# Keys and a quarter of the queries by seven products, their results stored by GpSimd's queue, and the plain stage in an order written by hand

## The chip, the core and the metric

The kernel runs on one core of a Trainium2 chip. A time is the device time of one execution in microseconds (us). In the profile PE is TensorE (matmuls), PEld its weight loads, DVE VectorE, ACT ScalarE, POOL GpSimd and SP the engine that does nothing but issue DMAs; POOL and ACT issue DMAs too, each in a queue of its own.

## What is computed

One layer of a bidirectional encoder, on 512 + 256 tokens (two requests, shared weights), all in float32:

```python
h = rmsnorm(x, ln_mix_g); z = h @ w_in              # 2048 -> 2560 columns
zf, q, k, v = z[:, :1024], z[:, 1024:2048], z[:, 2048:2304], z[:, 2304:]
of = fourier_mix(zf, w_f)                           # 8 groups of 128 channels
oa = window_attention(rope(q), rope(k), v, sink)    # 16 heads, 4 of keys, +-128 tokens
x = x + concat(rmsnorm(of), rmsnorm(oa)) @ w_out
u = relu(rmsnorm(x, ln_mlp_g) @ w_up); x = x + (u * u) @ w_down
y = rmsnorm(x, ln_final_g)
```

## The kernel before

Every float32 operand of a matmul is split into a high part (ScalarE copies it to float32r) and a low part (VectorE subtracts the high part), and a product is three matmuls: high x high, high x low, low x high. A matmul has 128 x 128 weights and 384 token columns (`HALF`).

`w_in` is worked off in blocks of 256 columns, `w_in[0]` to `w_in[9]`. Blocks 0 to 3 are the Fourier channels, 4 to 7 the queries, 8 the keys, 9 the values. The stages, in order:

- *Values* (block 9), to 41 us.
- *Product stage* (41 to 157.5 us): a pair of blocks against both halves of x (2 x 2 blocks of columns c and of the inner dimension k, and 2 x 2 blocks of x) by seven products of sums instead of eight products (`names7`: a11, s1, s2, s3, a22, s4, a12). Two pairs g are worked, blocks (0, 1) and (2, 3). A *piece* n is half of one product's inner dimension for one pair, 24 matmuls; there are 28, in the order product, pair, half e. For each piece the weights are loaded on SP (`load7`, five pieces ahead), in four of the seven products summed on VectorE (`sum7`, three ahead), split (`high7` on ScalarE, three ahead, `low7` on VectorE, two ahead) and multiplied (`product7`). The x operands are summed and split on the way (`high_at`, `low_at`: tables of the piece at which each step stands). Results are taken out of PSUM after a piece with e = 1 (`out7`), by a copy on ScalarE or an add on VectorE, and stored to DRAM (`zf_d`) from ScalarE's queue one piece later. Within it the sums of squares of x's rows are made (`row_load` on GpSimd's queue, `row_square`, `row_norms`, `row_turn`, `row_spread`), whose outcome `rb` scales every column.
- *Plain stage* (157.5 to 361.3 us): blocks 8, 6, 4, 5, 7 by ordinary products, four pieces each, 20 pieces of 48 matmuls. Between them TensorE does the Fourier groups (`fold`, `stage1`, `stage2`), placed by `after(piece, ...)`; a fraction .5 is the middle of the next piece. Keys and queries are rotated (`cross` on GpSimd, `turned` on VectorE), split and stored (`parts`). TensorE's order is the program's; that of the other engines is a scheduler's, but for the last piece.
- *Attention and the first output projection* (from 361.3 us), by a table of times; `proj_slot` needs pieces of `w_out` from `out_load` and `out_split`, of which 0 to 2 are split in the plain stage and 3 (`out_split(3)`) just behind it.
- The second half of the projection and the MLP.

DMAs of one queue are issued in order, and an engine that waits holds up all that stands behind in its program.

Of the kernel before, what the change touches and what calls it, by code (L numbers as in the profile page):

```python
# [40 lines left out]
def hybrid_encoder(ctx: ExitStack, tc: tile.TileContext, a: dict):  # L41
# [75 lines left out]
    kr_d = dpool.tile([4 * P, T], F32, tag="k", name="k")  # L117
    qr_d = [[dpool.tile([2 * P, T], F32, tag=f"q{c}{i}", name=f"q{c}{i}") for c in "hl"] for i in range(NKV)]
# [79 lines left out]
    with ExitStack() as ph:  # L198
        hp = ph.enter_context(tc.tile_pool(name="hp", bufs=1, reuse_waits="tile"))
        pp = ph.enter_context(tc.tile_pool(name="pp1", bufs=4, space=PSUM))  # L200
# [7 lines left out]
        NP7 = 4 * len(names7)  # L208
# [5 lines left out]
        def load7(n):  # L214
            if n >= NP7:
                return
            x, g, e = names7[n // 4], n // 2 % 2, n % 2
            blocks = blocks7.get(x, (x,))
            raw7[n] = []
            for i, x in enumerate(blocks):  # L220
                if n < 2 or i > 0 or (len(blocks) == 1 and e == 1):
                    raw = wpool.tile([P, 4, 256], F32, tag="raw", name="raw", bufs=2)
                else:
                    raw = hq["p"].tile([P, 4, 256], F32, tag="wr", name="wr", bufs=3)
                c, k = int(x[1]) - 1, int(x[2]) - 1
                k0 = 8 * k + 4 * e
                nc.sync.dma_start(raw[:], w_in[2 * g + c][:, k0 : k0 + 4, :])
                raw7[n].append(raw)

        def sum7(n):  # L230
            if n >= NP7:
                return
            s, ge = names7[n // 4], n % 4
            x = raw7[n][0]
            if s == "s1":
                kept7[ge] = hq["p"].tile([P, 4, 256], F32, tag="ws", name="ws", bufs=4)
# [28 lines left out]
        def product7(n):  # L265
            w, g, e = n // 4, n // 2 % 2, n % 2
            bank = bank7[names7[w]]
            opens = w == 0 or names7[w] in ("s1", "a12")
            wh, wl = w7.pop(n)
            if e == 0 and opens:  # L270
                for r in range(2):
                    ps7[bank, g, r] = pp.tile([P, 512], F32, **(dict(tag="f", bufs=4) if bank == "Y" and 2 * g + r < 4 else dict(tag="ps", bufs=4)), name="p7")
            x = xs[w % 2]
            for i in range(4):
                for r in range(2):
                    for q, (l, o) in enumerate(((wh, 0), (wh, 1), (wl, 0))):
                        nc.tensor.matmul(  # L277
                            ps7[bank, g, r][:, :HALF], l[:, i, r * P : (r + 1) * P], x[:, o, 4 * e + i, :],
# [4 lines left out]
        def out7(n):  # L283
            while put7:
                put7.pop(0)()
            if n < 0 or n % 2 == 0:
                return
            s, g = names7[n // 4], n // 2 % 2
            c, t, how = take7[s]
            for r in range(2):  # L290
                ps = ps7[bank7[s], g, r][:, :HALF]
                if how == 1:
                    z = c7.pop((c, t, g, r))
                    nc.vector.tensor_tensor(out=z[:], in0=ps, in1=z[:], op=ALU.add)
                else:
                    z = hq["p"].tile([P, HALF], F32, tag=f"z{c}{t}", name="z7", bufs=2 if how else 4)
                    nc.scalar.activation(z[:], ps, AF.Copy)
                if how == 0:
                    c7[c, t, g, r] = z
                else:  # L300
                    dst = zf_d[4 * g + 2 * c + r]
                    put7.append(lambda z=z, dst=dst, t=t: nc.scalar.dma_start(dst[:, t * HALF : (t + 1) * HALF], z[:]))
# [46 lines left out]
        for e in range(2):  # L349
            step(high_at, e, lambda e=e: xhigh(h1, b11, e))  # L350
            step(low_at, e, lambda e=e: xlow(l1, b11, h1, e))
            step(low_at, 2 + e, lambda e=e: xsum(b11, b22, b11, e))
            step(high_at, 4 + e, lambda e=e: xhigh(h0, b11, e))
            step(low_at, 4 + e, lambda e=e: xlow(l0, b11, h0, e))
            step(low_at, 7 + 2 * e, lambda e=e: difference(e))
            step(high_at, 8 + 2 * e, lambda e=e: xhigh(h1, fx["d"], e))
            step(low_at, 8 + 2 * e, lambda e=e: xlow(l1, fx["d"], h1, e))
            step(low_at, 11 + e, lambda e=e: xsum(b11, b21, b11, e))
            step(high_at, 12 + e, lambda e=e: xhigh(h0, b11, e))
            step(low_at, 13 + e, lambda e=e: xlow(l0, b11, h0, e))  # L360
            step(high_at, 16 + e, lambda e=e: xhigh(h1, b22, e))
            step(low_at, 16 + e, lambda e=e: xlow(l1, b22, h1, e))
            if e == 0:
                step(high_at, 18, second_block)
            step(high_at, 18 + e, lambda e=e: xhigh(fx["h12"], b12, e))
            step(low_at, 18 + e, lambda e=e: xlow(fx["l12"], b12, fx["h12"], e))
            step(high_at, 20 + e, lambda e=e: xhigh(h0, b21, e))
            step(low_at, 20 + e, lambda e=e: xlow(l0, b21, h0, e))
        step(low_at, 22, first_block)
        step(low_at, 20, lambda: first_load(0))  # L370
        for e in range(2):
            step(low_at, 24 + 2 * e, lambda e=e: first_split(e))
            if e == 0:
                step(low_at, 24, lambda: first_load(1))
        hq = {}

        with tc.tile_pool(name="xp", bufs=1, reuse_waits="tile") as xp, tc.manual_schedule(
# [63 lines left out]
            pv = [pp.tile([P, 512], F32, tag="f" if m < 4 else "ps", bufs=4, name="pv") for m in range(NM)]  # L441
# [24 lines left out]
            pw = pp.tile([P, 512], F32, tag="ps", bufs=4, name="pw")  # L466
# [60 lines left out]
        def row_turn():  # L527
            pr = raw7["r"] = pp.tile([P, 512], F32, tag="ps", bufs=4, name="pr0")
# [7 lines left out]

        with tc.tile_pool(name="hq", bufs=1, reuse_waits="tile") as hq["p"], tc.manual_schedule(
            engines={mybir.EngineType.SP, mybir.EngineType.Activation, mybir.EngineType.DVE}
        ):
            for n in range(2, 5):  # L540
                load7(n)
            high7(2)
            for n in range(NP7):
                for fn in high_at.get(n, ()):
                    fn()
                sum7(n + 3)
                high7(n + 3)
                low7(n + 2)
                for fn in low_at.get(n, ()):
                    fn()  # L550
                product7(n)
                out7(n - 1)
# [3 lines left out]
                if n in (12, 14, 16, 18):  # L556
                    for i in range(3 * n // 2 - 6, 3 * n // 2 - 3):
                        row_square(i)
                if n in (10, 12, 14, 16):
                    for i in range(3 * n // 2 - 3, 3 * n // 2):  # L560
                        row_load(i)
                if n == 18:
                    row_norms()
                if n == 21:
                    row_turn()
                if n == 24:
                    row_spread()
            out7(NP7 - 1)
            out7(-1)
# [5 lines left out]
        ssf = fp.tile([P, T], F32, tag="ssf", name="ssf")  # L575
        fst = {}
        def load_group(g):
# [4 lines left out]
            fst[g] = (z, wf)  # L582

        nc.sync.dma_start(cc[:], a["c_chan"])
        load_group(0)
        tabh = fp.tile([P, 4, 256], F32R, tag="tabh", name="tabh")
        tabl = fp.tile([P, 4, 256], F32R, tag="tabl", name="tabl")
        for i in range(2):
            tab = fp.tile([P, 2, 256], F32, tag="zf", name="tab", bufs=2)
            nc.sync.dma_start(tab[:], a["c_pos"][:, 2 * i : 2 * i + 2, :])  # L590
            split(tabh[:, 2 * i : 2 * i + 2, :], tabl[:, 2 * i : 2 * i + 2, :], tab[:])

        def fold(g):

            z, wf = fst.pop(g)
            nc.vector.tensor_tensor(out=z[:], in0=z[:], in1=rb[:], op=ALU.mult)
            pc = pp.tile([P, 512], F32, tag="f", bufs=4, name="pc")
            cw = fp.tile([P, 2, 2, P], F32R, tag="cw", name="cw", bufs=2)
            for i in range(2):
                nc.tensor.matmul(pc[:, i * P : (i + 1) * P], cc[:, i, :], wf[:], start=True, stop=True)  # L600
# [1261 lines left out]
```

## Time and profile before

| | us |
|---|---|
| runs: median (lowest to highest) of 3 | 2573.08 (2572.76 to 2573.61) |
| the profiled execution | 2573.4 |
| its span, first to last instruction | 2571.6 |
| TensorE busy | 2561.1 |
| VectorE busy | 1793.4 |
| ScalarE busy | 1121.7 |
| GpSimd busy | 242.9 |

A row of an instruction group reads: line, engine, operation, output<-inputs, their shapes, xcount | busy us in all, mean ns of one | idle time of the engine just before them, and what ended most of it. In rows of the timeline the start and the length come first. Ends of matmuls are modelled, so the distance from one start to the next tells more than a matmul's own length.

### The profile page before, as it was taken

What the parts mean: (1) busy time and instruction counts of PE and PEld (TensorE: products, weight loads), DVE (VectorE), ACT (ScalarE), POOL (GpSimd) and SP (SyncE); (2) the same over time, 40 slices, a digit from 0 to 9 for tenths busy, and PEclk for the clock granted to TensorE, in tenths of its full rate; (3) what the DMA queues carried; (4) which work ended last, traced back from release to release, by engine and by line L of the source; (5) the groups of instructions that cost most, each with busy time, mean ns of one, the idle gap of its engine ahead of it and who ended that gap; (6) DMA issues with size and microseconds to landing.
All of it is one profiled execution on the core that took longest, in us unless ns stands there. A gap on an engine that the chain in (4) does not pass through costs nothing.

```text
span 2571.6 us, 34801 instructions
## 1 busy us (share of the span) xinstructions
PE 2561.1 (100%) x13463; PEld 2345.3 (91%) x13463; DVE 1793.4 (70%) x2221; ACT 1121.7 (44%) x1622; POOL 242.9 (9%) x345
## 2 busy tenths in 40 slices
PE   9999999999999999999999999999999999999998
PEld 9999998888899999999999999988888888888887
DVE  8966468786465565656777777667766766777687
ACT  7644337674233333334445444433333333333335
POOL 0102322223201001100000000100000000000000
PEclk9999999999999999999999999999999999999999
DMA  8753567455655454456666666775543662554364
GB/s 305 234 182 122 178 186 207 142 165 191 222 178 181 154 174 168 164 190 239 218 227 230 213 217 214 266 285 176 175 154 121 216 227 85 175 185 158 101 210 153
DMA packets 259671, 487.84 MB, mean 190 GB/s; under 512 B 20586, under 2 KB 147056, under 8 KB 259248
## 3 DMA queue, kind: packets, MB, share of 16 engines
q1 hardware_dynamic: 187968, 321.77, 39.4%
q10 hardware_dynamic: 58512, 112.05, 11.5%
q0 software_dynamic: 13024, 51.79, 6.1%
q8 instruction: 106, 1.74, 0.3%
q14 instruction: 61, 0.50, 0.1%
HBM read 365.99 MB, written 119.54 MB: 189 GB/s over the span
## 4 chain that ended last, share of the span: by engine, by line
PE 97%; DVE 1%; DMA 1%; issue 0%; POOL 0%; SPq 0%; ACT 0%; POOLq 0%; DVEq 0%; ACTq 0%
PE pu L1229 36%; PE pd L1664 35%; PE pm L1082 10%; PE pz L835 5%; PE p L277 5%; PE pv L447 1%; PE o L960 1%; PE s L881 1%; PE t L938 1%; PE pe L664 0%; PE pa L643 0%; PE ptx L137 0%; DVE zs L729 0%; DMA raw<-in_w_out 0%; POOL zy L720 0%
## 5 line engine op out<-in xcount | busy, mean ns | idle before, releaser
L1229 PE MATMUL pu<-xf,wh 128*128 128x384 f32 x3072 | 780.2, 334 | 0.0
L1229 PEld LDWEIGHTS pu<-xf,wh 128*128 128x128 f32 x3072 | 554.2, 188 | 1.5 <-ACT o L1247 1.3
L1664 PE MATMUL pd<-wh,sh 128*128 128x512 f32 x1332 | 517.7, 389 | 0.0
L1664 PE MATMUL pd<-wl,sh 128*128 128x512 f32 x1332 | 517.7, 389 | 0.0
L1664 PE MATMUL pd<-wh,sl 128*128 128x512 f32 x1332 | 517.5, 389 | 0.0
L1229 PE MATMUL pu<-xf,wl 128*128 128x384 f32 x1536 | 513.1, 334 | 0.0
L1641 ACT ACTIVATE wh<-rd 128x1024 fp32r<-128x1024 f32 x200 | 202.3, 1054 | 522.3 <-PE pd L1664 422.0
L1651 DVE TENSOR_TENSOR wl<-rd,wh 128x1024 fp32r<-128x1024 f32 x200 | 236.0, 1221 | 226.4 <-ACT wh L1641 225.6
L1209 ACT ACTIVATE wh<-ur 128x1024 fp32r<-128x1024 f32 x160 | 170.1, 1063 | 382.6 <-PE pu L1229 207.9
L1664 PEld LDWEIGHTS pd<-wl,sh 128*128 128x128 f32 x1332 | 250.0, 188 | 51.9
L1664 PEld LDWEIGHTS pd<-wh,sl 128*128 128x128 f32 x1332 | 249.9, 188 | 52.0 <-DVE sl L1652 0.3
L1664 PEld LDWEIGHTS pd<-wh,sh 128*128 128x128 f32 x1332 | 250.0, 188 | 51.7
L1229 PEld LDWEIGHTS pu<-xf,wl 128*128 128x128 f32 x1536 | 288.3, 188 | 0.0
L1215 DVE TENSOR_TENSOR wl<-ur,wh 128x1024 fp32r<-128x1024 f32 x160 | 195.4, 1221 | 76.1 <-ACT wh L1209 76.1
L1250 DVE TENSOR_TENSOR o<-pu,o 128x768 f32<-128x768 f32 x160 | 152.8, 956 | 122.5 <-PE pu L1229 114.9
L1634 DVE TENSOR_TENSOR rd<-rd 128x1024 f32<-128x1024 f32 x112 | 131.7, 1217 | 0.0
L1229 PE MATMUL pu<-xs,wh 128*128 128x384 f32 x512 | 129.8, 334 | 0.0
L1209 ACT ACTIVATE wh<-sx 128x1024 fp32r<-128x1024 f32 x64 | 67.9, 1062 | 130.5 <-PE pu L1229 104.3
L277 PE MATMUL p<-xs,wh 128*128 128x384 f32 x448 | 113.7, 334 | 0.0
L1652 DVE TENSOR_TENSOR sl<-sr,sh 128x768 fp32r<-128x768 f32 x111 | 105.5, 951 | 0.0
L1215 DVE TENSOR_TENSOR wl<-sx,wh 128x1024 fp32r<-128x1024 f32 x64 | 78.2, 1222 | 23.8 <-ACT wh L1209 23.6
L1229 PEld LDWEIGHTS pu<-xs,wh 128*128 128x128 f32 x512 | 92.5, 188 | 0.0
(295 smaller groups left out, 3843.2 us busy)
## 6 DMA issues: line engine op xcount, KB each, us to landing
rd<-in_w_down SPq DMA_DIRECT2D x176, 512.0 KB, 5.2
ur<-in_w_up SPq DMA_DIRECT2D x128, 512.0 KB, 3.9
sr<-sd SPq DMA_DIRECT2D x95, 384.0 KB, 5.4
pd<-o ACTq DMA_DIRECT2D x60, 384.0 KB, 2.3
o<-pd POOLq DMA_DIRECT2D x60, 384.0 KB, 6.0
sd<-sm ACTq DMA_DIRECT2D x60, 384.0 KB, 2.8
raw<-in_w_in SPq DMA_DIRECT2D x39, 512.0 KB, 4.2
raw<-in_w_out SPq DMA_DIRECT2D x32, 512.0 KB, 4.7
```

The lines of the kernel that those rows point to most:

```text
L277: nc.tensor.matmul(ps7[bank, g, r][:, :HALF], l[:, i, r * P : (r + 1) * P], x[:, o, 4 * e + i, :], start=(opens and e == 0 and i == 0 and ...
L835: nc.tensor.matmul(ps[c][s][:, :HALF], w[:, i, cs], whole[j // 2][s][o][:, 4 * (j % 2) + i, :], start=first and n == 0, stop=stop and n == 2,)
L1082: nc.tensor.matmul(ps, l(k), w[:, k % 2, :], start=(k == 0 and n == 0), stop=(k == 7 and n == 2))
L1209: nc.scalar.activation(wh[:], raw[:], AF.Copy)
L1215: nc.vector.tensor_tensor(out=wl[:], in0=raw[:], in1=f32(wh[:]), op=ALU.subtract)
L1229: nc.tensor.matmul(ps[:, t, :HALF], w[:, i, t * P : (t + 1) * P], xb[:, o, i, :], start=(s == first_of[bank] and i == 0 and n == 0), stop= ...
L1250: nc.vector.tensor_tensor(out=o, in0=src, in1=o, op=ALU.add)
L1634: add = lambda x, y, op: nc.vector.tensor_tensor(out=x[:], in0=x[:], in1=y[:], op=op)
L1641: nc.scalar.activation(wh[:], t[:], AF.Copy)
L1651: nc.vector.tensor_tensor(out=wl[:], in0=t[:], in1=f32(wh[:]), op=ALU.subtract)
L1652: nc.vector.tensor_tensor(out=sl[:], in0=sr[:], in1=f32(sh[:]), op=ALU.subtract)
L1664: nc.tensor.matmul(o, l[:, q, ts], w[:, ns], start=(j == j0 and (q, t) == (0, 0)), stop=(j == j1 and (q, t) == (1, 2)),)
```

## The change

Block 8 (keys) and block 6 (a quarter of the queries) become a third pair of the product stage, which then has 42 pieces; the plain stage keeps blocks 4, 5 and 7, 12 pieces. Three details of the product stage change with it. Results of s1, s4 and a12 share two PSUM banks (`t`), the sums over a11, s2, s3 and a22 have six (`x`). A product's two row halves r are worked one after the other, and the first is taken out in the middle of its piece. And a11's result is stored and read back (`back7`) before a12 is added. All stores of results go through GpSimd's queue. The keys are rotated within the stage, at pieces 35 to 42 (`k_cross`, `k_turn`, `k_parts`). In the plain stage the order of SP, ACT, DVE and POOL is the program's throughout. Smaller parts: the row maximum is taken as a negated minimum, which saves one operation of one column per head, and the scratch of GpSimd's DMA descriptors is set to 4096.

```diff
+        cols7 = ((0, 1), (2, 3), (6, 8))
+        NS7 = 2 * len(cols7)
+        NP7 = NS7 * len(names7)
...
-            for i in range(4):
-                for r in range(2):
+            for r in range(2):
+                if e == 0 and opens:
+                    ps7[own, g, r] = pp.tile([P, 512], F32, tag="t" if own else "x", bufs=2 if own else 6, name="p7")
+                for i in range(4):
                     for q, (l, o) in enumerate(((wh, 0), (wh, 1), (wl, 0))):
...
+                put7.append(lambda: nc.gpsimd.dma_start(dst, z[:]))
+        def back7(g):
             for r in range(2):
+                z = c7[2, g, r] = tile7("z11", NS7)
+                nc.sync.dma_start(z[:], home7(g, 0, r)[:, :HALF])
...
+            for s, n in enumerate((36, 38, 40)):
+                step(k_at, n - 1, lambda s=s: k_cross(s))
+                step(k_at, n, lambda s=s: k_turn(s))
+                step(k_at, n, lambda s=s, n=n: k_parts(s, n))
+            step(k_at, 28, k_tables)
+            step(k_at, 33, k_loads)
+            step(k_at, 34, k_scale)
+            step(k_at, 34, k_keep)
             for n in range(NP7):
+                product7(n)
+                out7(n - 1, 1)
+                low7(n + 2)
+                out7(n, 0)
+                sum7(n + 3)
+                high7(n + 3)
                 for fn in high_at.get(n, ()):
                     fn()
-                sum7(n + 3)
-                high7(n + 3)
-                low7(n + 2)
                 for fn in low_at.get(n, ()):
                     fn()
-                product7(n)
-                out7(n - 1)
+                for fn in k_at.get(n, ()):
+                    fn()
+                stores7(1 if n % 2 else 0)
                 load7(n + 5)
...
+                if n in (33, 34, 35):
+                    back7(n - 33)
-                if n == 18:
+                if n == 24:
                     row_norms()
...
+                if n in (37, 39):
+                    piece_load((n - 37) // 2)
+                if n >= 40:
+                    piece_split(n - 40)
...
-            piece_split(piece + 2)
...
                 if c == 0:
                     for fn in todo.pop(piece - 0.5, ()):
                         fn()
+                    piece_split(piece + 2)
+            if piece == n_in - 1:
+                piece_split(piece + 3)
...
-    nc = bacc.Bacc("TRN2", target_bir_lowering=False, num_devices=1)
+    nc = bacc.Bacc("TRN2", target_bir_lowering=False, num_devices=1, dynamic_dma_scratch_size=4096)
```

VectorE's program in two pieces of the product s2, where the x operand for s3 is made (`wl` low parts of weights, `ws` and `wr` sums of weights, `d` and `xs` x operands, `z` results). Before, two pieces:

```order
L308 TENSOR_TENSOR d_1051<-xr_281,xr_279 128x1536
L246 TENSOR_TENSOR ws<-ws,raw 128x1024
L262 TENSOR_TENSOR wl<-ws,wh 128x1024
L314 TENSOR_TENSOR xs_283<-d_1051,xs_283 128x1536
L246 TENSOR_TENSOR wr<-wr,raw 128x1024
L262 TENSOR_TENSOR wl<-ws,wh 128x1024
```

Now, two pieces:

```order
L301 TENSOR_TENSOR z_1292<-p_793,z_1083 128x384
L257 TENSOR_TENSOR ws<-ws,wr 128x1024
L410 TENSOR_TENSOR xs_285<-d_1262,xs_285 128x1536
L301 TENSOR_TENSOR z_1327<-p_806,z_1117 128x384
L273 TENSOR_TENSOR wl<-ws,wh 128x1024
L257 TENSOR_TENSOR ws<-ws,raw 128x1024
L404 TENSOR_TENSOR d_1334<-xr_283,xr_281 128x1536
L273 TENSOR_TENSOR wl<-ws,wh 128x1024
```

Two results `z` have come between, one in each piece.

VectorE's program at the end of the product stage, where x operands of the plain stage are split (`xf`) and, now, keys are rotated (`kr`). Before:

```order
L294 TENSOR_TENSOR z_1186<-p_944,z_1186 128x384
L294 TENSOR_TENSOR z_1188<-p_945,z_1188 128x384
L262 TENSOR_TENSOR wl<-raw,wh 128x1024
L262 TENSOR_TENSOR wl<-wr,wh 128x1024
L73 SCALAR_TENSOR_TENSOR xf_1611<-d_1538,gall,xf_1610 128x384 x4
L294 TENSOR_TENSOR z_1261<-p_1014,z_1261 128x384
L294 TENSOR_TENSOR z_1263<-p_1015,z_1263 128x384
L262 TENSOR_TENSOR wl<-raw,wh 128x1024
```

Now, from piece 36 (its first result stands ahead) to the middle of 38:

```order
L273 TENSOR_TENSOR wl<-wr,wh 128x1024
L340 TENSOR_TENSOR kr<-kr 128x512
L342 TENSOR_TENSOR kr<-kr 128x256 x2
L273 TENSOR_TENSOR wl<-raw,wh 128x1024
L301 TENSOR_TENSOR z_2057<-p_2141,z_2057 128x384
L73 SCALAR_TENSOR_TENSOR xf_2037<-d_2046,gall,xf_2036 128x384 x4
L349 TENSOR_TENSOR kr<-kr 128x512
L301 TENSOR_TENSOR z_2059<-p_2154,z_2059 128x384
L273 TENSOR_TENSOR wl<-wr,wh 128x1024
L340 TENSOR_TENSOR kr<-kr 128x512
```

Results, keys and x operands alternate here, and each result is taken one by one.

VectorE's program at the plain stage's end: copies of the last sums (`zs<-pz`), low parts of `w_out` pieces (`wl<-raw`), low parts of the Fourier result (`ofl`). Before, from the last rotation (`zs` with `zh`, `zy`) over the low parts of output pieces 1 and 2 to the Fourier result:

```order
L746 SCALAR_TENSOR_TENSOR zs<-zs,zh 128x2x256 x2
L729 TENSOR_TENSOR zs<-zs,zy 128x256
L746 SCALAR_TENSOR_TENSOR zs<-zs,zh 128x2x256
L70 TENSOR_TENSOR wl<-raw,wh 128x1024 x2
L848 COPY zs<-pz 128x384 x2
L1066 TENSOR_TENSOR ofl_3923<-ofr,ofh_3922 128x512 x2
L896 ISA p,mx<-s,mask,sink 128x256
```

Now, from the low part of output piece 1:

```order
L909 TENSOR_SCALAR sink<-sink 128x16
L70 TENSOR_TENSOR wl<-raw,wh 128x1024
L979 COPY zs<-pz 128x384 x2
L70 TENSOR_TENSOR wl<-raw,wh 128x1024
L1194 TENSOR_TENSOR ofl_3977<-ofr,ofh_3976 128x512 x2
L1026 ISA p,nm<-s,mask,sink 128x256
L1026 ISA nm 128x1
```

The low part of output piece 2 has moved behind the copies. SP's queue at the same place, from output pieces 0 and 1 to 3 (`qs` are loads of queries, `ofr` of the Fourier result). Before:

```order
L188 DMA ofr<-ofd 128x4x128
L79 DMA raw<-in_w_out 128x2x512
L188 DMA ofr<-ofd 128x4x128
L766 DMA qs<-qh_81 64x4x128
L766 DMA qs<-ql_82 64x4x128
L766 DMA qs<-qh_81 64x4x128
L766 DMA qs<-ql_82 64x4x128
L766 DMA qs<-qh_83 64x4x128
L766 DMA qs<-ql_84 64x4x128
L766 DMA qs<-qh_83 64x4x128
L766 DMA qs<-ql_84 64x4x128
L79 DMA raw<-in_w_out 128x2x512
```

Now:

```order
L189 DMA ofr<-ofd 128x4x128 x2
L895 DMA qs<-qh_87 64x4x128
L895 DMA qs<-ql_88 64x4x128
L895 DMA qs<-qh_87 64x4x128
L895 DMA qs<-ql_88 64x4x128
L79 DMA raw<-in_w_out 128x2x512
L895 DMA qs<-qh_85 64x4x128
L895 DMA qs<-ql_86 64x4x128
L895 DMA qs<-qh_85 64x4x128
L895 DMA qs<-ql_86 64x4x128
L79 DMA raw<-in_w_out 128x2x512
```

Eight query loads stood between output pieces 2 and 3; now four do, and eight have been issued ahead of piece 2.

458 lines of the change are left out of this document (265 added, 193 removed).

## The prediction

> **What bounds the kernel now.** I read the page first (busy shares, chain), then busy time by stage, the chain in order of time, TensorE's waits, and at the end VectorE's groups in the product stage and the few microseconds around the plain stage's end.
>
> ```profile
> span 2571.6 us, 34801 instructions
> PE 2561.1 (100%) x13463; PEld 2345.3 (91%) x13463; DVE 1793.4 (70%) x2221; ACT 1121.7 (44%) x1622; POOL 242.9 (9%) x345
> ...
> PE 97%; DVE 1%; DMA 1%; issue 0%; POOL 0%; SPq 0%; ACT 0%; POOLq 0%; DVEq 0%; ACTq 0%
> ```
>
> TensorE is busy throughout and carries 97% of the chain that ended last. By stage (columns: window, length, then busy us of PE, PEld, DVE, ACT, POOL, then clock, DMA share, GB/s), the rows are the product stage, the plain stage with Fourier work, the plain stage with rotations, and the first attention slots:
>
> ```profile
> 40.90:157.50 116.60, 116.60 (x676) 116.51 (x675) 94.40 (x87) 70.86 (x99) 11.55 (x18) 1.00 0.66 220
> 157.50:285.00 127.50, 127.50 (x834) 127.30 (x833) 71.25 (x161) 55.95 (x143) 24.68 (x15) 1.00 0.41 133
> 285.00:361.30 76.30, 76.30 (x446) 76.30 (x446) 42.48 (x60) 21.59 (x33) 24.74 (x25) 1.00 0.61 205
> 361.30:384.00 22.70, 21.87 (x111) 17.67 (x110) 20.86 (x63) 13.14 (x32) 3.17 (x4) 1.00 0.70 205
> ```
>
> A busy TensorE could still be slow, so I check the pace of its matmuls in the chain (start, length, what) and its waits in the whole span (total, times, longest):
>
> ```profile
> 41.05 91.53 PE p L277 x528
> 132.69 24.97 PE p L277 x144
> ...
> 286.45 37.39 PE pz L835 x215
> ```
> ```profile
> PE pw L470 <- DVE ssx L132: 1.0, 1, 1.0
> PE pm L1082 <- DVE wl L70: 0.6, 1, 0.6
> ```
>
> 672 product matmuls take 116.5 us, 0.1735 us each; the plain ones 37.39 / 215 = 0.1739 us. Between 41 and 361 us TensorE waits for nothing that the profile names. The clock is 1.00 in all four rows. So a matmul of 128x384 that is taken away here is worth 0.174 us, provided that the engines that feed it keep up.
>
> **The change, part by part.**
>
> *Fewer matmuls.* Two column blocks of 256 leave the plain stage (4 pieces of 48 matmuls each, 384 in all) and become a third pair in the product stage (14 more pieces of 24 matmuls, 336). That is 48 fewer: 48 x 0.1735 = 8.3 us off the bounding engine. The Fourier, attention and MLP matmuls are the same ones.
>
> *VectorE in the product stage.* It grows from 28 to 42 pieces of 24 x 0.1735 = 4.16 us. What VectorE must do per piece:
>
> ```profile
> L314 DVE TENSOR_TENSOR xs<-xr,xs 128x1536 fp32r<-128x1536 f32 x10 | 17.5, 1752 | 3.4 <-ACT xs L311 3.2
> L262 DVE TENSOR_TENSOR wl<-wr,wh 128x1024 fp32r<-128x1024 f32 x11 | 13.4, 1218 | 8.0 <-ACT wh L254 8.0
> ...
> L294 DVE TENSOR_TENSOR z<-p,z 128x384 f32<-128x384 f32 x10 | 5.1, 548 | 0.0
> L246 DVE TENSOR_TENSOR ws<-wr,raw 128x1024 f32<-128x1024 f32 x4 | 4.9, 1220 | 1.0 <-DMA raw<-in_w_in 1.0
> ...
> L73 DVE SCALAR_TENSOR_TENSOR xf<-d,gall,xf 128x384 fp32r<-128x384 f32 x8 | 4.4, 614 | 7.8 <-ACT xf L72 7.8
> ```
>
> The weight work per piece is unchanged (a low part 1.22 us, in four of seven products a sum 1.22 us), but the work on x (1.75 us an operation) does not grow with the columns. Laid out piece by piece with these durations, the new stage needs 142 us of VectorE in 175 us; the old one by the same count 100 in 117, which the trace shows as 94.4, since neighbours overlap. The share falls from 86% to 81%. The worst stretch is s2 and s3: pieces 13 to 17, 19 and 20 hold a low part, a sum, one result (0.55) and one operation on x, 4.73 us against 4.16, so VectorE falls behind by 0.57 each, at most 2.9 us. The old table reaches 2.3 us (two results in pieces 10 and 12), and TensorE did not wait. Since a low part is ready nearly two pieces ahead of its use, some 7 us are covered. Cost: 0.
>
> *PSUM turnover.* s1, s4 and a12 now share two banks, so the second row half of a new pair must wait until the old pair's second result is taken, 2.08 us (12 matmuls) after its last matmul. Taking it is queued in VectorE behind what the previous piece left. The tightest place is piece 37: low part 1.22, result at half time (2.08 to 2.6), four low parts of x (4 x 0.61), K's low part (0.68): done 5.8 us after its start, the second result at 6.3, which is 2.2 us into piece 38, against 2.08. At piece 34 it is 1.6. So 0.2 us, from 0 below (no earlier stage waited) to about 1.4 above, when K's third rotation product falls on the same moment:
>
> ```profile
> L729 DVE TENSOR_TENSOR zs<-zs,zy x28: 411/418/965, 294.1 to 372.1; 128x256 f32<-128x256 f32 x28
> ```
>
> The same operation takes 0.42 us alone and 0.965 beside GpSimd's products; two such hits give the 1.2 us. [...] I take 0.7, the middle.
>
> *Stores by GpSimd's queue.* 16 stores leave ScalarE's queue and 30 (six of them of a11, which are read back by six loads in SP's queue at pieces 33 to 35) stand in GpSimd's, between row loads.
>
> ```profile
> zf<-z ACTq DMA_DIRECT2D x14, 192.0 KB, 4.7
> d<-in_x_sample POOLq DMA_DIRECT2D x8, 256.0 KB, 6.6
> rb<-r0d POOLq DMA_DIRECT2D x1, 384.0 KB, 8.2
> ```
>
> A store takes 2 us longer to land by these rows. The first Fourier group's last store is issued in piece 38, lands by 40, and its fold stands in the middle of the first plain piece (43): hidden by three pieces. K's store of piece 30 lands by 32, its load stands at 33, ahead of the weights of pieces 39 to 41: hidden by one piece, and by the pieces loaded ahead. The row factor is issued near 30.5, lands at 32.5, and is used at 34. Cost 0; if GpSimd's queue is late, the DVE reduction of the row sums (piece 24) is the first to stand.
>
> *Plain stage.* 12 pieces instead of 20, Fourier work still one group per piece. With Fourier work VectorE was 71 of 127 us busy; three rotations of about 3 us each come into the eight Fourier pieces, so about 70%, and each TensorE step uses parts made at least half a piece (4.2 us) earlier. From 0 to 1.5 us; I take 0, as that window shows no wait.
>
> *The plain stage's end.* The only named wait of the old middle lies here:
>
> ```profile
> 358.26 6.54 DMA raw<-in_w_out
> ...
> 364.88 1.07 ACT wh L69
> ...
> 365.98 1.33 DVE wl L70
> ```
> ```profile
> 359.00 1.23 DVE L70 TENSOR_TENSOR wl<-raw,wh 128x1024 fp32r<-128x1024 f32 x1 [5.29 <-ACT wh L69]
> 361.30 1.02 DVE L848 COPY zs<-pz 128x384 f32<-128x384 f32 x2 [1.08 <-PE pz L835]
> 362.24 1.28 DVE L1066 TENSOR_TENSOR ofl<-ofr,ofh 128x512 fp32r<-128x512 f32 x2
> ```
> ```profile
> 357.14 0.86 ACT L848 COPY zs<-pz 128x384 f32<-128x384 f32 x2 [4.70 <-PE pz L835]
> ```
> ```profile
> 363.60 1.07 PE L1084 MATMUL pm<-wh,ofl 128*128 128x512 f32 x4
> ...
> 366.36 0.39 PE L1082 MATMUL pm<-wh,ofh 128*128 128x512 f32 x1
> 367.36 0.50 PE L1082 MATMUL pm<-wl,ofh 128*128 128x512 f32 x1 [0.61 <-DVE wl L70]
> ```
>
> Call the stage's end E (361.3 here). Two things move. First, the low part of output piece 2 goes from ahead of the two copies to behind them: the first `ofl` is then done at E + 1.0 + 1.2 + 0.6 (the first half of 1.28) = E + 2.8 instead of 1.6, and TensorE asks for it at 363.60, E + 2.3: 0.5 us. Second, output piece 1 is split in the middle of the last piece, behind ScalarE's copies (which ended at 358.0, E - 3.3) and a DMA issue: high part until about E - 1.7, low part until E - 0.5, and only then can SP load output piece 3, at E - 0.5 instead of E - 3.0. From landing to TensorE took 367.36 - 364.80 = 2.56 us. If the load takes 6.5 us as here, TensorE goes on at E + 8.6 instead of E + 6.06: 2.5 us lost. But in the old order 12 q loads and three more surrounded this load; in the new one 8 of the 12 are issued a piece earlier, and the usual time is shorter:
>
> ```profile
> raw<-in_w_out SPq DMA_DIRECT2D x32, 512.0 KB, 4.7
> ```
>
> With 4.7 us it is E + 6.8, 0.7 us lost, and the 0.5 above disappears in it; with less, up to 0.8 won. I take 0.8 (nearer the median of 32), ends -0.8 and 2.6.
>
> *Attention.* 96 VectorE operations of one column go; no row shows TensorE waiting for VectorE between 384 and 578, so 0. MLP: unchanged.
>
> Sum against the profiled execution, 2573.4 us (its span is 2571.6): -8.3 + 0.7 + 0.8 = -6.8, so 2566.6; the median of the runs shown, 2573.08, lies 0.3 lower, so 2566.3 us. 0.2% (5.1 us) is about what a measurement of this kernel can tell from no change.
>
> **Rivals.**
>
> *More is lost at the joints.* Load of output piece 3 as slow as here (2.6), piece 38's wait at its upper end (1.4), and the Fourier end (1.5): 5.5 instead of 1.5, 2570.3 us. For it: the DMA engines are at 0.70 there. Against: fewer loads collide. 0.18.
>
> *VectorE becomes the bound of the product stage.* If every GpSimd DMA issue (45 in the stage; 0.54 us by the row below) held VectorE up as the rotation's products did, its 142 us become 166 of 175. The stretch of pieces 13 to 20 (9 row loads, 2 stores) then falls behind by 2.9 + 11 x 0.54 = 8.8 us, 1.8 more than the 7 covered, and the joint in piece 38 is at its upper end: 2568.8 us. Against: the low parts above have a mean of 1218 ns, with GpSimd's loads running among them. 0.08.
>
> *GpSimd's queue stalls, slower than before.* The diff also sets the scratch of GpSimd's DMA descriptors to 4096.
>
> ```profile
> L1733 POOL DMA_DIRECT2D acc<-x x24: 537/539/544, 1655.5 to 1681.5; - x24
> ...
> DMA to landing us min/median/max: 5.2/9.8/10.6
> ```
>
> There 24 are issued in 26 us, 1.13 apart, and land after 9.8: about eight in flight. If that number comes from the scratch and falls to two, the 18 DMAs of pieces 16 to 24 (12 row loads, 6 stores) take 18 x 6.6 / 2 = 59 us in 33 us: 26 late. VectorE stands at the reduction of piece 24, and after 7 us of lead TensorE does: 19 us, 2585 us. With three in flight 6.6 us are late and nothing is lost; two decides it. Against: in the program each of these DMAs waits for the eighth before it, which alone gives eight. [...] 0.07.
>
> *Nothing is lost, or the end gains:* 2573.1 - 8.3 - 0.5 to + 0.5, 2564.8 us: 0.13. My forecast has the rest: 0.52, its own range 2565.3 to 2568.2.
>
> **Numbers.** Faster by over 0.2% (under 2567.9): 0.49 of the forecast's 0.52, 0.13, and 0.05 of the first two rivals: 0.67. Slower by over 0.2% (over 2578.2): the queue rival, 0.07, and 0.01 for what I did not see. The rest, 0.25, is within. Low 2564.2 leaves out 0.06 (a gain at the end); high 2572.0 leaves out the slow rival and some of the joints, 0.12.
>
> **What would show it.** TensorE: 1008 product and 576 plain matmuls at 0.1735 us; the plain stage begins near 41 + 175 = 216 us and ends near 353.5. Product stage right: no TensorE wait of over 1.5 us, the largest near 200 us (piece 38), for a result `z`. Joint right: output piece 3 issued about 0.5 us before the last plain matmul, a wait for `wl` of 1 to 2 us behind it. Queue right: GpSimd's DMAs up to eight in flight, the row-sum reduction idle under 5 us. The prediction is wrong if the pace of the product matmuls itself rises, if waits for `wl` or `wh` appear inside the product stage, or if the later stages, which are not touched, take another time.

## The result, and the profile after

The changed kernel takes 2588.74 us (median of 4 runs, 2588.27 to 2589.54) against 2573.35 before: ratio 1.006, interval 1.0043 to 1.0078. It is 15.4 us slower. The forecast was 2566.3, its range 2564.2 to 2572.0.

The page and TensorE's waits of the changed kernel:

```profile
span 2587.3 us, 34692 instructions
PE 2558.9 (99%) x13415; PEld 2341.8 (91%) x13415; DVE 1809.0 (70%) x2152; ACT 1125.9 (44%) x1622; POOL 266.8 (10%) x385
...
PE 94%; issue 2%; DVE 2%; ACT 1%; DMA 1%; POOL 0%; ACTq 0%; SPq 0%; DVEq 0%; POOLq 0%
```
```profile
PE pm L1210 <- ACT ofh L1193: 10.1, 1, 10.1
PE p L287 <- ACT rb L629: 5.2, 1, 5.2
PE s L1011 <- DMA ofr<-ofd: 2.2, 1, 2.2
```

TensorE's share of the chain fell from 97 to 94%, and three waits have come: of the first output matmul for the high part of the Fourier result (`ofh`), of a product piece put down to the row factors (`rb`), and of the first score matmul (`s`), put down to a Fourier load (`ofr`). By stage (window, length, busy us of PE, PEld, DVE, ACT, POOL, clock, DMA share, GB/s): the product stage, the plain stage, the joint from the last plain to the first output matmul; then three pieces of 5 us: the wait at 170 us and what follows it.

```profile
40.70:225.50 184.80, 178.74 (x1012) 177.21 (x1011) 135.17 (x136) 87.73 (x117) 38.05 (x63) 0.98 0.72 247
225.50:363.90 138.40, 137.47 (x892) 137.15 (x892) 91.57 (x193) 60.33 (x149) 44.66 (x36) 1.00 0.44 149
363.90:377.10 13.20, 0.89 (x5) 0.36 (x4) 4.34 (x9) 4.11 (x7) 3.43 (x5) 0.67 0.88 242
...
169.90:174.90 5.00, 0.00 (x0) 0.00 (x0) 3.88 (x4) 2.95 (x5) 0.54 (x1) 0.89 0.82 246
174.90:180.00 5.10, 5.08 (x16) 5.08 (x17) 3.65 (x3) 2.78 (x3) 1.65 (x3) 0.50 0.45 146
180.00:185.00 5.00, 5.00 (x29) 5.00 (x28) 2.35 (x4) 1.06 (x1) 0.60 (x2) 0.94 0.94 272
```

Set against the forecast, in us of the profiled executions (forecast: 1008 x 0.1735 and 0.7; 203.6 less 384 x 0.1739; 353.7 and 0.8; both2 is the fastest kernel of the experiments):

| stretch | before | forecast | changed | both2 |
|---|---|---|---|---|
| product stage | 116.6 | 175.6 | 184.8 | 174.9 |
| plain stage | 203.6 | 136.8 | 138.4 | 139.4 |
| last plain matmul to the MLP | 353.7 | 354.5 | 367.1 | 358.3 |
| all else | 1897.7 | 1897.7 | 1897.0 | 1897.1 |

So against the forecast about 9 us are lost in the product stage and 13 at the joint. In the product stage TensorE stands still for 6.1 us (184.80 less 178.74 busy), and most of the rest is the lower clock behind its longest wait: 0.50 for 5.1 us is 2.5 us.

**What the product stage shows.** Take the start of TensorE's piece n less the end of VectorE's `wl` of that piece, and call it the lead. In the changed kernel it is 7.7 us at piece 15, 2.6 at 16, 2.8 at 17, -0.6 at 18, and about 0 up to 24 and at 27, 28 and 30; before, it never fell under 4.3 from piece 9 on. VectorE and ScalarE where it is lost:

```profile
109.01 1.22 DVE L257 TENSOR_TENSOR wr<-wr,raw 128x1024 f32<-128x1024 f32 x1
112.81 1.76 DVE L410 TENSOR_TENSOR xs<-d,xs 128x1536 fp32r<-128x1536 f32 x1 [2.58 <-ACT xs L407]
```
```profile
110.34 1.06 ACT L265 ACTIVATE wh<-wr 128x1024 fp32r<-128x1024 f32 x1 [3.34 <-DVE wr L257]
111.31 1.47 ACT L407 ACTIVATE xs<-d 128x1536 fp32r<-128x1536 f32 x1
```

VectorE makes a sum; ScalarE, which waited for it, makes the weight's high part and then x's; only then can VectorE make x's low part. It stands idle for 2.58 us with work behind it. The same group before and now (busy, mean ns | idle ahead of it):

```profile
L314 DVE TENSOR_TENSOR xs<-d,xs 128x1536 fp32r<-128x1536 f32 x2 | 3.5, 1746 | 0.0
```
```profile
L410 DVE TENSOR_TENSOR xs<-d,xs 128x1536 fp32r<-128x1536 f32 x2 | 3.5, 1759 | 5.2 <-ACT xs L407 5.2
```

Before, the loop gave ScalarE x's high part first and VectorE the low part of weights between the sum and x's low part.

**What the joint shows.** SP's queue and ScalarE's program of the changed kernel, around the last plain matmul at 363.9:

```profile
351.83 0.33 SPq L879 DMA_DIRECT2D kd<-k  x1
353.20 0.61 SPq L895 DMA_DIRECT2D qs<-qh  x1
361.70 0.52 SPq L895 DMA_DIRECT2D qs<-ql  x1
...
365.99 0.63 SPq L895 DMA_DIRECT2D qs<-qh  x1
369.40 0.51 SPq L895 DMA_DIRECT2D qs<-ql  x1
370.01 0.55 SPq L79 DMA_DIRECT2D raw<-in_w_out  x1
```
```profile
366.64 1.07 ACT L69 ACTIVATE wh<-raw 128x1024 fp32r<-128x1024 f32 x1
375.44 1.06 ACT L69 ACTIVATE wh<-raw 128x1024 fp32r<-128x1024 f32 x1 [7.72 <-DMA raw<-in_w_out]
...
376.40 1.13 ACT L1193 ACTIVATE ofh<-ofr 128x512 fp32r<-128x512 f32 x2
```

Output piece 2 (370.01) is loaded 6 us behind the stage's end; query loads that themselves wait stand ahead of it. Its buffer had come free at 359.2, when the low part of output piece 0 was done, so 10.8 us of the delay are the queue. ScalarE stands at its split, with `ofh`, whose data landed at 368, behind it. In the kernel before the same two loads stood here:

```profile
313.12 0.33 SPq L754 DMA_DIRECT2D kd<-k  x1
```
```profile
346.29 0.37 SPq L79 DMA_DIRECT2D raw<-in_w_out  x1
```

That is 48 us (keys) and 15 us (output piece 2) ahead of the end at 361.3.

### The profile page after: what moved, and what is told of

Same layout as the page of the kernel before. It is cut to its first block, busy times and chain, and to the rows that moved or that the text cites. A ratio compares the mean times of both kernels' runs of the same rounds, so it can differ in the third digit from the quotient of the medians.

```text
span 2587.3 us, 34692 instructions
## 1 busy us (share of the span) xinstructions
PE 2558.9 (99%) x13415; PEld 2341.8 (91%) x13415; DVE 1809.0 (70%) x2152; ACT 1125.9 (44%) x1622; POOL 266.8 (10%) x385
## 4 chain that ended last, share of the span: by engine, by line
PE 94%; issue 2%; DVE 2%; ACT 1%; DMA 1%; POOL 0%; ACTq 0%; SPq 0%; DVEq 0%; POOLq 0%
PE pu L1357 36%; PE pd L1792 35%; PE pm L1210 10%; PE p L287 4%; PE pz L970 3%; PE pv L543 1%; PE s L1011 1%; PE o L1088 1%; PE t L1066 1%; PE ptx L138 0%; PE pa L789 0%; PE pe L810 0%; PE pm L1212 0%; DMA d<-in_x_sample 0%; ACT xs L407 0%
## 5 line engine op out<-in xcount | busy, mean ns | idle before, releaser
L287 PE MATMUL p<-xs,wh 128*128 128x384 f32 x672 | 172.8, 338 | 5.2 <-ACT rb L629 5.2
L287 PEld LDWEIGHTS p<-xs,wh 128*128 128x128 f32 x672 | 122.8, 190 | 5.6 <-ACT rb L629 5.5
L287 PE MATMUL p<-xs,wl 128*128 128x384 f32 x336 | 113.7, 338 | 0.9 <-DVE wl L273 0.7
```

Source lines behind the costliest of these rows:

```text
L287: nc.tensor.matmul(ps7[own, g, r][:, :HALF], l[:, i, r * P : (r + 1) * P], x[:, o, 4 * e + i, :], start=(opens and e == 0 and i == 0 and q ...
```

## Experiments

Each was timed beside the kernel before, which had medians of 2572.8 to 2573.4. Single runs of the changed variants scatter by about 2 us either way, so stage lengths from their traces tell more than small differences of the medians.

**Queue or feeders, and the joint's order.** My first theory was the queue of the slower rival with another cause: row loads behind stores.

*pool_manual*: `engines={..., DVE}` becomes `engines={..., DVE, Pool}` for the product stage.

> The changed kernel with GpSimd's instructions of the product stage kept in the order of the code (in the changed kernel a scheduler orders them), so that the three row loads of piece 18 stand ahead of the first result of s3 instead of behind it; the number of DMAs in its queue is the same. Theory A (a row load stands in the queue behind a store that waits for its result): the fourth row load goes out near 117 us instead of 129.9, the row-sum reduction on VectorE comes near 143 instead of 152.6, TensorE's wait of 5.4 us at 169 us and the lower clock behind it go, 2579 to 2581 us instead of 2588.7. Theory B (the queue holds too few descriptors, or a store takes too long): same DMAs, same wait, 2587 to 2590. Theory C (VectorE has too much work in the product stage): 2587 to 2590, and the reduction no earlier.

2589.05 us. The fourth row load went out at 129.76, no earlier: it waits for ScalarE's square of the row whose buffer it takes, and ScalarE is late. The wait for `rb` stays 5.2. Theory A is refuted.

*stores_act*: `nc.gpsimd.dma_start(dst, z[:])` becomes `nc.scalar.dma_start(dst, z[:])`.

> The changed kernel with the results z of the product stage stored by ScalarE's queue, as before the change. Theory A (order in GpSimd's queue): row loads have that queue to themselves, no TensorE wait near 169 us, 2578 to 2581 us. Theory B (too few descriptors in GpSimd's queue): the same gain. Theory C (VectorE overloaded): 2587 to 2590. If ScalarE, which now stands at each store until VectorE has made the result, is late with its high parts, part of the gain is lost again: 2582 to 2586.

2590.80 us, `rb` 5.2: neither the order nor the number of the DMAs in GpSimd's queue sets this wait. The changed kernel's own trace speaks against the descriptor scratch of 4096 as a cause too. The 24 additions in the MLP that showed about eight in flight before land after a median of 9.9 us now, against 9.8; the change without that setting was not run:

```profile
L1861 POOL DMA_DIRECT2D acc<-x x24: 537/537/546, 1671.6 to 1699.0; - x24
...
DMA to landing us min/median/max: 5.4/9.9/11.6
```

*turns_early*: `turns` at (1, 2, 3), (4, 5, 6), (7.5, 8, 8.5).

> The changed kernel with the nine query rotations of the plain stage two to three half pieces earlier (pieces 1, 2, 3; 4, 5, 6; 7.5, 8, 8.5 instead of 1, 3, 5; 7, 8, 8.5; 9, 9.5, 10). Theory D (at the plain stage's end the last rotations wait for the landing of a store that shares the DMA engines with the key load, and the query loads and the load of output piece 2 stand behind them in SP's queue): the stores have landed before the key load of piece 9, output piece 2 is issued near 361 instead of 370 us, TensorE's 10.1 us at the joint shrink to 1 to 4, 2579 to 2583 us. Theory E (the key load of 1.5 MB, pulled to the end because the Fourier tiles free its place only then, is itself in the way): the joint keeps 6 us or more, 2584 to 2587. If VectorE has no room for rotations beside the Fourier groups, waits appear between 230 and 340 us and eat the gain.

2591.58 us. The joint shrank from 13.2 to 7.3 us, but the plain stage grew from 138.4 to 145.4, with a wait for `cw` in nearly every Fourier piece:

```profile
PE pm L1210 <- ACT ofh L1193: 6.1, 1, 6.1
PE pa L789 <- DVE cw L70: 5.5, 6, 1.5
```

The rotations have no room there. Theory D is half right.

*q_late*: `load_q(2)` and `load_q(1)` from 9.5 and 10.5 to 11, behind the output loads.

> The changed kernel with the query loads of units 1 and 2 put behind the loads of output pieces 2 and 3 in SP's queue; rotations as they are. Theory D1 (the load of output piece 2 is late because it stands behind query loads): it goes out near 364 instead of 370 us, the joint's wait falls by 5 to 7 us, 2581 to 2584 us. Theory D2 (the wait comes from the late rotation on VectorE and ScalarE, which split the output pieces behind it): ScalarE's split of output piece 1 stays at 366.6, the gain is under 2 us, 2586.5 to 2589.

2585.82 us, between the two forecasts. Output piece 2 went out at 364.4 and the joint fell from 13.2 to 8.1 us (theory D1), 1.3 came back in the attention stage. ScalarE's split of output piece 1 stayed where it was (366.2), as D2 said.

**Which part of the lateness.**

*pr_bank*: `tag="t", bufs=2, name="pr0"` becomes `tag="x", bufs=6, name="pr0"`.

> The changed kernel with one PSUM tile moved: the transposed row factors (pr) take a bank of tag x instead of one of the two banks of tag t, which s4 needs when it opens (piece 30). Theory P (TensorE's 5.4 us at 169 us is a wait for that bank, which ScalarE frees only where row_spread stands in its program, behind the x work of piece 29; it was 5.2 to 5.4 in four kernels whatever stood in GpSimd's queue): the wait goes, and the 2.5 us of lower clock behind it with it, 2580 to 2582 us instead of 2588.7. Theory F (VectorE and ScalarE are simply late; the bank is only where it shows): TensorE stops instead for weights wl or wh of pieces 30 to 32, 2586 to 2589.

2586.62 us. The wait for `rb` is gone, but TensorE waits 3.2 us for a result `z` and 1.3 for `wh` instead; the stage takes 185.4. The bank was only where the lateness showed. That is theory F, but for the place: it expected the wait at weights, and most of it came at a result.

*sum_first*: `sum7(n + 3)` ahead of `out7(n, 0)`.

> The changed kernel with two lines of the product loop swapped: VectorE's sum of the weights of piece n + 3 ahead of the first result of piece n, instead of behind it. In the trace of the changed kernel the low part of a piece is ready 7.7 us ahead of TensorE's start of it up to piece 15, 2.6 at 16 and 0 from 18 to 30. Theory L (the lead is lost because the sum waits for TensorE's half of piece n, and high part, x operand and low parts follow it one behind the other on two engines): the lead at pieces 18 to 24 is over 2 us, the waits for wl inside the stage (0.7 and some smaller) go, 2585.5 to 2588. Theory V (VectorE has too many us of work there): lead and time as they were, 2588 to 2590.

2587.28 us; the stage in the trace 180.1 instead of 184.8, the lead at 18 to 24 1.4 to 2.3 instead of 0, `rb` 3.4 instead of 5.2. Theory L, in part: the lead is under the 2 us that it asked for, and the total did not show all of the stage's gain.

*kd_split*: `load_k(0, 256)` at its place, `load_k(256, 768)` at 11.

> The changed kernel with the key load of 1.5 MB split by tokens: the first 256 (which the first four units need) at its place, the other 512 behind the query loads at the end of the plain stage; same bytes. Theory E (the key load takes the DMA engines for 9 us, so that the rotation stores and query loads around it land 9 us late, and what waits for them in SP's, GpSimd's and ScalarE's programs is late): stores of 353 us land in 4 to 6 us, output piece 2 goes out 3 to 6 us earlier, the joint (last plain to first output matmul) falls from 13.2 to 6 to 10 us, 2582 to 2586. Theory D1 alone (only the order in SP's queue): the joint stays over 11, 2587 to 2590.

2585.37 us; the joint 7.9 instead of 13.2, the rotation store that landed after 8.8 us now 5.5 (theory E).

*combo1*: pr_bank, q_late and kd_split.

> The bank of pr, the split key load and the query loads of units 1 and 2 behind output pieces 2 and 3, together. If the causes add up: 2588.7 - 7.9 (bank and clock) - 5 (queue order, measured alone) - 2 to 3 (key load) = 2573 to 2575 us, level with the kernel before. If the joint has another wait behind the ones removed (the first query load, or the split of output piece 1 behind the last rotation), 2576 to 2579.

2585.89 us, far over either forecast. The joint is 3.6, but 6 us came back behind it (ScalarE's next `ofh` late by 3.8), and the product stage kept its loss. Measured singly the three gave 2.1, 2.9 and 3.4 us; together they give 2.9. So the gains of single repairs do not add up here. The run *joint* below, which changes ScalarE's order too and puts two loads later, gets more out of the same end.

**The loop's order by itself, in both kernels.**

*x_first*:

```
 product7(n)
+x high parts (high_at)
 out7(n - 1, 1)
-low7(n + 2); out7(n, 0)
 sum7(n + 3); high7(n + 3)
-x high parts (high_at)
+low7(n + 2); out7(n, 0)
 x low parts (low_at)
```

> The changed kernel with the product loop in the order of the kernel before, the results put in: x's high part ahead of the weights' sum and high part, then low part, result, x's low part. In the changed kernel VectorE's low part of x stands right behind its sum and waits 2.58 us for ScalarE, which makes the weight's high part (1.06) and then x's (1.47); this falls on pieces 13 and 15, where the lead of the weights drops from 7.7 to 2.6 and from 2.8 to -0.6. Theory L (the loop's order made two engines wait for each other): the lead stays over 3 us from 16 to 30, all waits of the product stage go (5.4 for rb, the rest 1 to 2, the lower clock behind them 2.5), stage 175 to 177 instead of 184.8 us, 2579 to 2581 us. Theory V (too much VectorE work): lead near 0 again by piece 20, stage over 182, 2586 to 2589. Theory P (the bank of pr alone): the 5 us for rb stay.

2579.46 us. The stage is what its matmuls take, and VectorE no longer waits for x's high part:

```profile
40.80:215.60 174.80, 174.80 (x1010) 174.71 (x1010) 134.75 (x136) 87.50 (x117) 38.61 (x63) 1.00 0.76 261
215.60:354.90 139.30, 137.57 (x893) 137.18 (x892) 92.49 (x193) 60.24 (x149) 45.62 (x36) 1.00 0.44 148
354.90:369.30 14.40, 0.85 (x5) 0.35 (x3) 4.22 (x9) 4.03 (x7) 3.40 (x5) 0.60 0.88 242
```
```profile
L410 DVE TENSOR_TENSOR xs<-d,xs 128x1536 fp32r<-128x1536 f32 x2 | 3.5, 1747 | 0.0
```

VectorE's work is the same (134.75 against 135.17); the lead is at least 2.4 from piece 16 to 30, less than the 3 that theory L asked for, but enough. Stage and time are those of theory L; V and P are refuted.

*before_x_last*: the kernel before, with `low7, sum7, high7, x high, x low` in its loop.

> The kernel before with its product loop in the order of the changed kernel (low part, sum, weight's high part, then x's high and low part); nothing else of the change, its results stay one piece late. Theory L: VectorE waits about 2.6 us at each of its x low parts that follow a sum, the lead falls by 5 us or more from 4.3 to 5 us at pieces 9 to 13, and TensorE waits for weights, 1 to 6 us more than 2572.8: 2574 to 2579. If the lead just covers it, 2572.5 to 2573.5; theory V has no reason for any change.

2591.55 us: 18.2 us slower than before, three times the most that I had expected, and in the product stage alone (133.9 instead of 116.6):

```profile
40.70:174.60 133.90, 122.25 (x676) 120.28 (x675) 94.51 (x87) 69.40 (x98) 11.54 (x18) 0.96 0.57 191
```
```profile
L314 DVE TENSOR_TENSOR xs<-xr,xs 128x1536 fp32r<-128x1536 f32 x10 | 17.6, 1757 | 15.9 <-ACT xs L311 15.8
...
L314 DVE TENSOR_TENSOR xs<-d,xs 128x1536 fp32r<-128x1536 f32 x2 | 3.5, 1758 | 5.2 <-ACT xs L311 5.2
```

VectorE is as busy as before (94.51 against 94.40 us), but its idle time in the stage went from 22.2 to 39.4 us, as much as the stage grew; ahead of the first of these groups it is 15.9 us where the prediction's row had 3.4. TensorE's waits are for weights, as expected, and for a result that ScalarE takes out late:

```profile
PE p L277 <- DVE wl L262: 7.8, 4, 2.2
PE p L277 <- ACT z L297: 3.9, 1, 3.9
```

The order alone does it, without a third pair, new banks or new stores. Why it costs twice as much here as in the changed kernel was not followed up; the work on x falls on 28 pieces here and on 42 there.

*joint*: split key load (rest at attention step 8), `load_q(1)` at 11, `load_q(2)` at step 1, `out_split(2)` behind `split_of(0)`.

> The changed kernel with the end of the plain stage alone mended: the first 256 tokens of the keys loaded at their place and the rest later, query loads of units 1 and 2 behind output pieces 2 and 3, and on ScalarE the split of the Fourier result ahead of that of output piece 2. Theory: TensorE waits at the joint because (1) output piece 2 is loaded after the stage instead of 15 us ahead of its end, behind query loads, and (2) ScalarE stands at its split with the Fourier result behind it, while the key load slows all of them. With all three taken away the span from the last plain to the first output matmul falls from 13.2 to 2 to 4 us, a wait of 1 to 4 us for output piece 2 remains behind it, 2579 to 2582 us. If the load of output piece 2 itself decides (its buffer comes free only when output piece 0 is split), the wait moves behind the first matmuls and 6 us remain: 2582 to 2585.

2581.69 us; the joint 2.1 instead of 13.2, 2.3 more in the attention stage. The time and the joint are as forecast. The run takes all three causes away at once: q_late and kd_split show the queue's order and the key load by themselves, while the order on ScalarE was not run alone. Against combo1 this run has that order and two later loads more, and where combo1 got back 6 us behind the joint, it gets back 2.3.

*both*: x_first and joint.

> The loop order of x_first and the joint of the run before it, together. If the two causes are separate and add up: 2588.7 - 8 to 9 - 7 to 9 = 2571 to 2574 us, level with the kernel before or 1 to 2 us under it; if the joint's wait is set by the loads' landing after an earlier end of the stage, it grows again and the sum stays at 2574 to 2577.

2573.37 us, ratio 0.9998 (0.9989 to 1.0008): the repairs gave 9.3 and 7.1 us each alone and give 15.4 together, 1 us less than their sum and the whole difference to the kernel before. The causes are separate.

**What of the 8.3 us is still missing.**

*both2*: both, and output pieces 0, 1 and 2 split at the start of pieces 10 and 11 and in the middle of 11.

> The loop order and the joint of the last run, and the splits of output pieces 0, 1, 2 half a piece to a piece earlier (0 at the start of piece 10, 1 at the start of 11, 2 in its middle), so that output pieces 2 and 3 are loaded 12 and 7 us ahead of the stage's end. Theory S (what is left at the joint, 360.3 us from the last plain matmul to the MLP against 353.7 before, is output pieces split and loaded late because the new plain stage splits in the middle of a piece): the waits for wh and wl behind the joint (4 us in all) go, 355 to 357 us for that stretch, 2567.5 to 2570 us. Theory E (the DMA engines are too full there with any order): the waits move to query and Fourier loads, 2571 to 2574.

2572.09 us, ratio 0.9997 (0.9988 to 1.0007). The waits for `wh` and `wl` behind the joint are gone; the stretch to the MLP is 358.3 instead of 360.3, not the 355 to 357 of theory S. What is left:

```profile
PE pm L1212 <- ACT ofh L1195: 2.1, 1, 2.1
PE pa L789 <- DVE cw L70: 1.7, 2, 1.3
PE s L1013 <- DMA qs<-ql: 1.6, 1, 1.6
```

The interval of both2 holds 1, so even this kernel is not shown to be faster than the one before. In the traces it is 1.9 us shorter: of the 8.3 us, 2.6 go to the plain stage (139.4 against the forecast's 136.8) and 4.6 to the stretch behind it (358.3 against 353.7). There the waits for `ofh` and for a query load, and the lower clock behind the first of them (1.7 us, below), add up to 5.4 us, which covers it.

*both2_kd*: both2 with the key load whole.

> As the last, but the key load whole again at its place (1.5 MB at piece 9, 10 us ahead of the end). Theory E: it costs 3 us or more against the last run. Theory S: under 2 us, since the output pieces are now loaded with time to spare.

2575.00 us, 2.9 more, from the joint (6.8 instead of 3.1): about what theory E asked for.

*split_early*: x_first with the early splits alone.

> The changed kernel with the loop order and the early splits of output pieces 0, 1 and 2 alone; queries, keys and the Fourier split where the change has them (x_first has 14.4 us from the last plain to the first output matmul, 2579.5 us). Theory S: that span falls to under 5 us, 2569 to 2572. If the order in SP's queue counts as much (output piece 3 and the Fourier loads behind queries that wait for rotations), 2573 to 2577.

2577.51 us: the joint 6.9 instead of 14.4, but 4 us come back in the attention stage. Early splits alone are worth 2 us; the order in SP's queue counts too.

*both3*: both2 with `ofr` ahead of the first queries, the rest of the keys at step 17, pair 1 turned at 1.5, 3.5, 5.

> both2 with three more moves: the Fourier load of the joint ahead of the first query load in SP's queue (in both2 ScalarE's ofh waits for it until 357.4, 2.4 us after the last plain matmul), the other 512 tokens of the keys 9 attention steps later (in both2 they share the DMA engines with the rotation stores that unit 3's queries wait for: 1.7 us at 380.6), and the first two query rotations half a piece later (in both2 the low part of the rotation stands in VectorE ahead of the Fourier weights cw and waits for ScalarE; TensorE 1.5 and 0.5 us). If each wait goes and no other comes: 2572.1 - 1.5 - 1.7 - 2 = 2567 us, 5 to 6 under the kernel before. If the waits move to the next load at the joint (output piece 3, the second query load), 2569 to 2572.

2574.71 us, a miss. The plain stage grew to 142.9, with new waits in later Fourier pieces; the joint did not shrink (3.5). Three moves went in at once, so which of them cost what is open.

## Why the prediction was wrong

- **Fewer matmuls, -8.3:** right in mechanism and size. The pace stayed 0.1735 us, and x_first's stage of 174.8 us is 1008 of them. The losses came elsewhere.
- **VectorE in the product stage, 0:** this step failed, by 9 to 10 us (184.8 against the forecast's 175.6 and x_first's 174.8). Its count was of busy time, and that was right (142 counted, overlaps included; 135.2 measured). But it took a work list for a schedule: 4.73 us against 4.16 a piece leaves out that two engines, each in the order of its program, hand each other parts. The order fences ahead of the prediction show the low part of weights gone from between sum and x's low part; I read only the added results there. Two waits of 2.58 us, the excess of 0.57 a piece and sums that stand behind a result of TensorE's half piece used up the 7 us of cover, which had been there (7.7 at piece 15). The order as a whole is shown to be the cause (x_first, before_x_last). How the loss divides among these three was not measured, but for the last: sum_first gave back 1.4 to 2.3 us of lead. The rival that GpSimd's DMA issues slow VectorE down named the right engine, but not the cause: low parts of weights took 1.22 us as before.
- **PSUM turnover, 0.7 near piece 38:** wrong place, wrong tile. The wait came at piece 30, 5.2 us, for the bank of the transposed row factors, which I had not counted among the users of tag t. With the engines in time it costs nothing (x_first has no such wait), so it belongs to the term above. In the sum for the upper end, two hits of 0.965 against 0.418 are 1.1 us, not 1.2.
- **Stores by GpSimd's queue, 0, and the slower rival:** the cost was right (pool_manual, stores_act). The rival's sign came true and its number nearly (2585), but that is luck, for its cause did not: about eight DMAs are still in flight in the MLP (24 issued in 27.4 us, landing after a median of 9.9). That the scratch of 4096 leaves two in flight was an assumption of mine; no run shows it.
- **Plain stage, 0 of 0 to 1.5:** 1.6 in the changed kernel, 2.5 in x_first, of which 0.9 and 1.7 are named waits for `cw`, the weights of a Fourier group. In both2 the longest stands behind a rotation on both engines: ScalarE's high part of it waited 2.42 us for VectorE, then VectorE's low part 0.70 us for ScalarE.
- **The joint, 0.8 of -0.8 to 2.6:** this step failed, by 12 us. I followed the load of output piece 3 and took that of piece 2 as unmoved, though its buffer comes free only when piece 0 is split, here at 359.2. I counted the eight query loads ahead of it as relief; they were the queue in front of it. And I did not see that the shorter plain stage, with the eight Fourier pieces still in it, moves the key load from 48 to 12 us ahead of the end.
- **Attention and MLP, 0:** right, within 0.7.

## To carry to other kernels

Where engines hand parts to each other in turn, sum waits as well as work: write the hand-overs of one step down for both engines in their order, since one operation moved behind another's input can cost more than the work added. When a stage gets shorter, list every load that was hidden in its end and ask where each stands now, what frees its buffer, and what is ahead of it in its queue. A wait names where lateness shows; to find where it began, follow the lead of the feeder piece by piece.

## What the runs showed of the hardware

A wait of TensorE cost more than its length in several of these runs. After the 5.2 us at 170 us the granted clock was 0.50 for 5.1 us, so 2.5 us more; in pr_bank, after 3.2 us, 0.50 for 5.1; in both2, after two short waits (0.2 and 2.1 us) within 3 us at the joint, 0.65 for 4.9 us, 1.7 us more. But in both3 the clock stayed at 1.00 after waits of 2.3 and 0.3 us within 3.5. The first row is of both2, the second of both3:

```profile
358.10:363.00 4.90, 4.86 (x16) 3.97 (x17) 4.43 (x10) 2.24 (x5) 3.71 (x4) 0.65 1.05 308
```
```profile
361.70:364.00 2.30, 2.30 (x11) 1.96 (x12) 2.30 (x5) 0.43 (x1) 1.69 (x2) 1.00 0.83 212
```

So the slow stretch was as long behind the wait of 3.2 us as behind that of 5.2; what sets its length and depth these runs do not show. None of the prediction's terms had this.

A key load of 1.5 MB took 9.2 us to land, and a store of 256 KB issued just behind it 8.8 instead of 2.1 to 2.6, as five such stores did earlier in the plain stage. GpSimd's next rotation product, which needed that store's buffer, waited 7.6 us, so here a load held up an engine that never reads it.
